# HGRN2 score levels on 64-column halves of TensorE, the diagonal as its own product on the same halves, the last level with half of the keys

## Chip, core and metric

The kernel runs on one core of a Trainium2 chip. The metric is the device time of one launch in microseconds (us). Three runs of the kernel before gave 2126.46 to 2127.39 us, median 2127.11.

## What is computed

Two layers of a decoder trunk, 512 tokens, width 1024, all in float32. Each layer has a SwiGLU network, a mixer, and a second SwiGLU network, with RMS norms around each. The mixer has one projection into everything it needs, a gated linear recurrence with four heads (HGRN2), a sliding-window attention with eight heads, and a gated sum of the two. The change lies in the recurrence. Per head, with keys and queries of 128 channels, the reference computes in chunks of 64 tokens:

```python
def step(state, inp):
    qb, kb, vb, gb = inp
    G = jnp.cumsum(gb, axis=2)
    o_inter = jnp.einsum('bhtd,bhde->bhte', qb * jnp.exp(G), state)
    diff = G[:, :, :, None, :] - G[:, :, None, :, :]
    decay = jnp.exp(jnp.where(causal[:, :, None], diff, -jnp.inf))
    scores = jnp.einsum('bhtd,bhtsd,bhsd->bhts', qb, decay, kb)
    o = o_inter + jnp.einsum('bhts,bhse->bhte', scores, vb)
    G_last = G[:, :, -1:, :]
    new_state = (jnp.exp(G_last[:, :, 0, :])[..., None] * state
                 + jnp.einsum('bhsd,bhse->bhde', kb * jnp.exp(G_last - G), vb))
    return new_state, o
```

So the score of query t and key s is a sum over channels of q(t) k(s) times the product of the forget gates f between s and t, for every s up to t.

## The kernel before

Activations lie with features on the 128 partitions and 512 tokens along the free dimension. Weights stream from DRAM in tiles of 128 x 1024 (`Stream`). ACT casts each tile to a rounded part `whi` (L321), and DVE (L328), or a DMA that POOL issues (L326), makes the rest `wlo`. A product of the large layers is then three matmuls (`mm3`). All matmuls go through `mm` (L115), all transposes through L122.

PE's instructions keep the order in which the program issues them. The other engines' orders are made by a scheduler. The program's own planner `Order` mixes the attention and the recurrence, which are generators, into the stream of weight products. It adds up an estimated PE time `order.t`. When a generator yields a delay from the table `WAIT`, it becomes due that much later, and the next call of `poll` after that runs it to its next yield. So PE does projections while DVE and ACT prepare the next product of a head.

PSUM has eight banks, of 512 float32 columns on 128 partitions each: five called `acc` (projections) and three called `aux` (everything small), each handed out in turn. Tiles of 128 x 512 in SBUF are called `s` (61 of them).

`recurrence_scores` (L938) makes one head's scores, which `mixer` calls through `head` and `run`. `q` and `kz` are a head's queries and keys, `f` the gates, `qa` starts as q times f. `TT` = 4 blocks of 128 tokens are worked on at the same time. Its steps:

- Diagonal (L945 to L952): four products of 128 keys by 128 queries, of which only the diagonal is wanted. DVE multiplies by the identity (L949) and writes the score tile `sd`.
- Levels b = 1, 2, 4, 8, 16, 32, taken in three pairs (L991). At level b, every second group of b queries meets the group of b keys just before it. `meet(b)` multiplies the odd groups of `qa` (L984) and the even groups of `kz` (L986) by products of gates, and halves the list of products `prod` (L988). `mv` holds three lots of 64 query columns for each block: those of level b, those of level 2b, and those of level 2b with a further gate for the far half of the keys (L1000). One product for each block (L1006) has 128 keys as the stationary operand and these 192 columns as the moving one. Two blocks fill a bank, so a pair of levels takes two `aux` banks. `place` (L970 to L976) then copies the wanted entries into `sd` with a mask, three times for each bank.
- Level 64 (L1016 to L1025): the second 64 queries of each block against all 128 keys, and a masked copy that keeps the first 64 keys.
- Then products between blocks (L1030 and L1041), which the change leaves as they are.

`run` multiplies the scores with the values into one bank, normalizes, gates and transposes. Heads 0 and 1 run beside the attention's projections, heads 2 and 3 later in the same mixer. In `attend`, the products at L1137 and L1189 already work on halves of the array.

Of the kernel before, what the change touches and what calls it, by code (L numbers as in the profile page):

```python
# [7 lines left out]
F32 = mybir.dt.float32  # L8
F32R = mybir.dt.float32r
I32 = mybir.dt.int32  # L10
AF = mybir.ActivationFunctionType
ALU = mybir.AluOpType
# [3 lines left out]
P = 128  # L16
# [4 lines left out]
TT = S // P  # L21
# [7 lines left out]
MASKS = [(m, n) for b in LEVELS[:-1:2] for m, n in ((b, b), (2 * b, 2 * b), (2 * b, b))] + [(64, 64)]  # L29
SLOTS = 61  # L30

WAIT = dict(
    early=0.0, first=0.0, spread=2300.0, squares=1700.0, lay=34500.0, laid=770.0, normed=7600.0, final=2600.0,
    head=2600.0, diag=0.0, level=1720.0, chunks=1270.0, blocks=350.0, norm=2370.0, gate=8000.0,
    values=1200.0, scores=2000.0, exp=9000.0, shares=4500.0, turn=1900.0, turned=3000.0, rest=1200.0, lent=3500.0, apart=4000.0, block=2000.0, pair=4000.0, att0=1260.0, att1=12300.0,
)
W32, WS, AHEAD, TAIL, PLAIN, FIRST, EARLY, LATE = 4, 6, 3, 4, 4, 7, 4, 8
# [8 lines left out]
def trunk(ctx: ExitStack, tc: tile.TileContext, xin, wall, gains, lbT, hgain, sinks, c_dist, c_mask, c_ident, out):  # L46
    nc = tc.nc
    cp = ctx.enter_context(tc.tile_pool(name="cp", bufs=1))
    sb = ctx.enter_context(tc.tile_pool(name="sb", bufs=1))
# [9 lines left out]
    def nm(s):  # L59
        seq[0] += 1  # L60
        return f"{s}_{seq[0]}"

    def big(dt=F32, shape=None):
        return sb.tile(shape or [P, S], dt, tag="s", name=nm("s"), bufs=SLOTS)
# [7 lines left out]
    def aux():  # L72
        return ps.tile([P, S], F32, tag="aux", name=nm("aux"), bufs=3)

    def const(shape, name, dt=F32):
        return cp.tile(shape, dt, tag=name, name=name)
# [35 lines left out]
    order = Order()  # L112

    def mm(o, lhsT, rhs, start, stop):
        nc.tensor.matmul(o, lhsT, rhs, start=start, stop=stop)  # L115
        n = 1
        for d in rhs.shape[1:]:
            n *= d
        order.t += max(n / 2.4, 27.0) * 4 if rhs.dtype == F32 else max(n / 2.4, 107.0)

    def transpose(o, src):
        nc.tensor.transpose(o, src, ident)  # L122
# [15 lines left out]
    p = aux()  # L138
    for _ in range(15):
        mm(p[:, :P], ones, ones, True, True)  # L140
# [12 lines left out]
    class Stream:  # L153
# [195 lines left out]
        def next(self, n=1, uses=1):  # L349

            c = self.c
            assert c + n <= 8
            it = self.need(self.cur)
            it.left += n * (uses - 1)
            self.c = (c + n) % 8
            if self.c == 0:
                self.cur += 1
            return it, n, it.hi[:, c * P : (c + n) * P], it.lo[:, c * P : (c + n) * P]
# [18 lines left out]
    def mm3(o, st, mv, start, stop):  # L377

        mm(o, st[0], mv[0], start, False)
        mm(o, st[0], mv[1], False, False)  # L380
        mm(o, st[1], mv[0], False, stop)
# [556 lines left out]
    def recurrence_scores(q, f, kz, box):  # L938

        qa = big()
        nc.vector.tensor_tensor(qa, q, f, op=ALU.mult)
        sd = big(F32, [P, TT, P])
        p0 = aux()  # L945
        for c in range(TT):
            cs = slice(c * P, (c + 1) * P)
            mm(p0[:, cs], kz[:, cs], q[:, cs], True, True)
        nc.vector.tensor_tensor(  # L949
            sd, p0.rearrange("p (c t) -> p c t", c=TT), ident.unsqueeze(1).to_broadcast([P, TT, P]), op=ALU.mult  # L950
        )
        yield WAIT["diag"]  # L952
        pr = big()
        prod, off = f, 0

        def halves(t, b):

            v = t.rearrange("p (n two b) -> p n two b", two=2, b=b)
            return v[:, :, 0, :], v[:, :, 1, :]

        def odd(t, b):
            return t.rearrange("p (c n two b) -> p c n two b", c=TT, two=2, b=b)[:, :, :, 1, :]

        def dense(t, b):
            return t.rearrange("p c (n b) -> p c n b", b=b)

        def spread(v, b):
            return v.to_broadcast([P, v.shape[1], b])

        def place(b, m, src, c):  # L970

            nc.vector.copy_predicated(
                sd.rearrange("p c (n two b) -> p c n two b", two=2, b=b)[:, c, :, 1, :],
                mask[:, m, :].rearrange("p (n b) -> p n b", b=b).unsqueeze(1).to_broadcast([P, 2, 64 // b, b]),
                dense(src, b),
            )  # L976

        def meet(b):

            nonlocal prod, off  # L980
            n = S // (2 * b)
            pv = prod.rearrange("p (n two) -> p n two", two=2)
            kv, qw = halves(kz, b)[0], halves(qa, b)[1]
            nc.vector.tensor_tensor(qw, qw, spread(pv[:, :, 0:1], b), op=ALU.mult)  # L984
            yield
            nc.vector.tensor_tensor(kv, kv, spread(pv[:, :, 1:2], b), op=ALU.mult)  # L986
            nxt = pr[:, off : off + n]
            nc.vector.tensor_tensor(nxt, pv[:, :, 0], pv[:, :, 1], op=ALU.mult)  # L988
            prod, off = nxt, off + n

        for i, b in enumerate(LEVELS[:-1:2]):  # L991


            mv = sb.tile([P, TT, 192], F32, tag="tt", name=nm("mv"), bufs=2)
            nc.scalar.copy(dense(mv[:, :, :64], b), odd(qa, b))
            first = meet(b)
            next(first)
            nc.scalar.copy(dense(mv[:, :, 64:128], 2 * b), odd(qa, 2 * b))
            way = prod.rearrange("p (c n four) -> p c n four", c=TT, four=4)[:, :, :, 1:2]
            nc.vector.tensor_tensor(  # L1000
                dense(mv[:, :, 128:], 2 * b), odd(qa, 2 * b), way.to_broadcast([P, TT, P // (4 * b), 2 * b]), op=ALU.mult
            )
            yield WAIT["pair"]
            lv = [aux()[:, :384].rearrange("p (c t) -> p c t", c=2) for _ in range(2)]
            for c in range(TT):
                mm(lv[c // 2][:, c % 2, :], kz[:, c * P : (c + 1) * P], mv[:, c, :], True, True)  # L1006
            next(first, None)
            for _ in meet(2 * b):
                pass
            for j, v in enumerate(lv):  # L1010
                c = slice(2 * j, 2 * j + 2)
                place(b, 3 * i, v[:, :, :64], c)
                place(2 * b, 3 * i + 1, v[:, :, 64:128], c)
                place(2 * b, 3 * i + 2, v[:, :, 128:], c)
            yield WAIT["level"]
        b = LEVELS[-1]  # L1016
        lv = aux()
        for c in range(TT):
            mm(lv[:, c * b : (c + 1) * b], kz[:, c * P : (c + 1) * P], qa[:, c * P + b : (c + 1) * P], True, True)
        for _ in meet(b):  # L1020
            pass
        v = lv[:, :256].rearrange("p (c t) -> p c t", c=TT)
        for j in range(2):
            c = slice(2 * j, 2 * j + 2)
            place(b, len(MASKS) - 1, v[:, c, :], c)  # L1025
        yield WAIT["level"]

        s1 = big(F32, [P, 2, P])
        p1 = aux()
        for i, (s, t) in enumerate(((0, 1), (2, 3))):  # L1030
            mm(p1[:, i * P : (i + 1) * P], kz[:, s * P : (s + 1) * P], qa[:, t * P : (t + 1) * P], True, True)
        for s, t in ((0, 1), (2, 3)):
            ks, qt = kz[:, s * P : (s + 1) * P], qa[:, t * P : (t + 1) * P]
            nc.vector.tensor_scalar(ks, ks, prod[:, t : t + 1], None, op0=ALU.mult)
            nc.vector.tensor_scalar(qt, qt, prod[:, s : s + 1], None, op0=ALU.mult)
        nc.scalar.copy(s1, p1[:, : 2 * P].rearrange("p (c t) -> p c t", c=2))
        yield WAIT["chunks"]

        s2 = big(F32, [P, 2, 2 * P])
        p2 = aux()  # L1040
        for s in range(2):  # L1041
            mm(p2[:, s * 256 : (s + 1) * 256], kz[:, s * P : (s + 1) * P], qa[:, 256:512], True, True)
        nc.scalar.copy(s2, p2.rearrange("p (c t) -> p c t", c=2))

        def block(s, t):
            if s == t:
                return sd[:, s, :]
            if (s, t) in ((0, 1), (2, 3)):
                return s1[:, s // 2, :]
            return s2[:, s, (t - 2) * P : (t - 1) * P]  # L1050

        box.append(block)
        yield WAIT["blocks"]

    def mixer(l, pre, nxt):
# [3 lines left out]
        def head(i, ph, pq):  # L1059
# [8 lines left out]
            def run():  # L1068
                yield WAIT["head"]
                box = []  # L1070
                yield from recurrence_scores(q, f, k, box)
                if len(vs) < TT:
                    while len(vs) < TT:
# [196 lines left out]
    for l in range(DEPTH):  # L1270
        for n in (0, 2, 4):
# [5 lines left out]
            else:  # L1277
                p = FIRST if l + n == 0 else PLAIN
# [10 lines left out]
    ident = const([P, P], "ident")  # L1289
    nc.sync.dma_start(ident, c_ident)  # L1290
    dist = const([P, 256], "dist")
    nc.sync.dma_start(dist, c_dist)
    mask = const([P, len(MASKS), 64], "mask", I32)
    nc.sync.dma_start(mask, c_mask)
    lb_in = const([P, DEPTH, H], "lb_in")
    nc.sync.dma_start(lb_in, lbT)
    hgh = const([P, DEPTH, P], "hgh")
# [136 lines left out]
```

## Time and profile before

| | us |
|---|---|
| median of three runs | 2127.11 |
| profiled execution, first to last instruction | 2123.9 |
| PE busy | 2110.6 |
| DVE busy | 1573.4 |
| ACT busy | 1119.0 |
| PE waits for other engines, in total | 9.1 |

The profiler records one execution. Busy time is the union of an engine's instructions. A matmul's record begins when it is issued and ends, by a model, when its last result is written, so records of successive matmuls overlap; what one costs is seen in the distance between starts. PEld is the loading of stationary operands. A float32 product leaves two such records, and a product of the rounded parts leaves one. In a row such as `128*64 128x512`, the first pair is the rows and columns of the array that are used (keys' channels by stationary columns), the second the moving operand. A bracket at the end of a row is idle time before it and what ended it. The recurrence's levels of heads 0 and 1 lie at 387 to 433 us in the first layer and 1437 to 1483 us in the second, those of heads 2 and 3 at 517 to 574 us and 1567 to 1624 us. The granted clock of TensorE was 0.999 over the span.

### The profile page before, as it was taken

The page shows a single profiled execution, that of the slowest core. Times are in us where ns is not written, and L with a number is a line of the kernel's source. Part 1 is how long each engine was busy: PE and PEld are TensorE (multiplying, and loading weights), DVE is VectorE, ACT ScalarE, POOL GpSimd, SP SyncE. Part 2 cuts the span into 40 slices and gives each one's busy share as a digit, 9 for nine tenths or more (in the row PEclk, how much of TensorE's full clock was granted, in tenths as well). Part 3 has the DMA queues.
Part 4 walks back from the last instruction along what each step waited for, and adds up shares of the span by engine and source line. Part 5 has one row for each costly group of instructions (what it writes and reads, how often), then busy time and mean ns, then how long its engine had stood idle before and what let it go on. Part 6 is the DMA issues. An engine that isn't in the chain of part 4 may idle for free.

```text
span 2123.9 us, 34765 instructions
## 1 busy us (share of the span) xinstructions
PE 2110.6 (99%) x13293; PEld 1898.1 (89%) x13293; DVE 1573.4 (74%) x2793; ACT 1119.0 (53%) x1884; POOL 152.2 (7%) x180
## 2 busy tenths in 40 slices
PE   9999999999999999999999999999999999999998
PEld 8899988887888999998899998898778989999987
DVE  5877886768776777789587778767687757777884
ACT  7555555346445555556455556453554545555562
POOL 0011000000000011110001110000000000111000
PEclk9999999999999999999999999999999999999999
DMA  8677663221236357774447775632122463677751
GB/s 251 149 185 182 167 181 118 92 67 64 66 100 208 120 125 176 182 197 123 153 113 177 183 183 141 197 119 80 60 70 60 124 194 110 149 180 182 185 158 51
DMA packets 146870, 298.48 MB, mean 141 GB/s; under 512 B 15664, under 2 KB 73488, under 8 KB 146704
## 3 DMA queue, kind: packets, MB, share of 16 engines
q1 hardware_dynamic: 121216, 228.31, 32.7%
q0 software_dynamic: 25344, 67.91, 18.6%
q8 instruction: 104, 1.70, 0.3%
q14 instruction: 62, 0.51, 0.1%
q10 hardware_dynamic: 144, 0.05, 0.0%
HBM read 213.58 MB, written 14.73 MB: 107 GB/s over the span
## 4 chain that ended last, share of the span: by engine, by line
PE 75%; DVE 7%; ACT 3%; issue 1%; DMA 1%; SPq 0%; ACTq 0%; DVEq 0%
PE acc L115 55%; PE aux L115 19%; DVE s L398 1%; PE aux L122 1%; ACT whi L321 1%; DVE wlo L283 1%; DMA w<-wall 1%; DVE wlo L328 1%; PE acc L122 1%; ACT s L397 1%; DVE tt L265 0%; DVE w L264 0%; DVE s L273 0%; DVE w L274 0%; ACT whi L278 0%
## 5 line engine op out<-in xcount | busy, mean ns | idle before, releaser
L115 PE MATMUL acc<-s,whi 128*128 128x256 f32 (+1 forms) x4968 | 1068.8, 312 | 0.7 <-DVE s L901 0.7
L115 PEld LDWEIGHTS acc<-s,whi 128*128 128x128 f32 x4968 | 810.1, 191 | 48.7 <-issue 3.7
L115 PE MATMUL acc<-s,wlo 128*128 128x256 f32 (+1 forms) x2484 | 770.2, 310 | 0.1
L115 PEld LDWEIGHTS acc<-s,wlo 128*128 128x128 f32 x2484 | 474.1, 191 | 26.0 <-DVE wlo L328 0.4
L321 ACT CAST whi<-w 128x1024 fp32r<-128x1024 f32 (+1 forms) x341 | 316.6, 947 | 242.0 <-PE aux L115 100.2
L115 PE MATMUL acc<-whi,s 128*128 128x512 f32 x1264 | 414.5, 394 | 0.0
L321 ACT CAST whi<-tt 128x1024 fp32r<-128x1024 f32 x154 | 161.4, 1048 | 337.7 <-DVE tt L315 199.5
L328 DVE TENSOR_TENSOR wlo<-w,whi 128x1024 fp32r<-128x1024 f32 (+1 forms) x181 | 218.5, 1216 | 135.3 <-ACT whi L321 131.6
L115 PEld LDWEIGHTS acc<-whi,s 128*128 128x128 f32 x1264 | 237.1, 188 | 55.7 <-issue 3.2
L328 DVE TENSOR_TENSOR wlo<-tt,whi 128x1024 fp32r<-128x1024 f32 x154 | 188.1, 1222 | 101.6 <-ACT whi L321 101.6
L326 POOL DMA_DIRECT2D wlo<-w x160 | 138.2, 865 | 1723.5 <-ACT wlo L325 1363.1
L115 PE MATMUL acc<-wlo,s 128*128 128x512 f32 x632 | 246.7, 390 | 1.2 <-DVE wlo L283 1.2
L115 PE MATMUL aux<-s,whi 128*128 128x256 f32 x1232 | 225.1, 283 | 0.0
L115 PE MATMUL aux<-whi,s 128*128 128x512 f32 x592 | 196.7, 390 | 0.0
L115 PEld LDWEIGHTS aux<-s,whi 128*128 128x128 f32 x1232 | 192.2, 192 | 0.0
L115 PE MATMUL aux<-s,wlo 128*128 128x256 f32 x616 | 174.3, 283 | 0.0
L115 PEld LDWEIGHTS acc<-wlo,s 128*128 128x128 f32 x632 | 118.8, 188 | 25.5 <-DVE wlo L283 2.4
L115 PEld LDWEIGHTS aux<-whi,s 128*128 128x128 f32 x592 | 111.2, 188 | 22.9
L325 ACT ACTIVATE wlo<-w 128x1024 fp32r<-128x1024 f32 (+1 forms) x160 | 129.8, 844 | 0.0
L397 ACT CAST s<-s 128x512 fp32r<-128x512 f32 (+1 forms) x164 | 88.4, 580 | 75.8 <-DVE s L456 72.2
L115 PEld LDWEIGHTS aux<-s,wlo 128*128 128x128 f32 x616 | 118.3, 192 | 0.0
L115 PE MATMUL aux<-wlo,s 128*128 128x512 f32 x296 | 115.2, 389 | 0.0
(182 smaller groups left out, 2189.1 us busy)
## 6 DMA issues: line engine op xcount, KB each, us to landing
w<-wall SPq DMA_DIRECT2D x267, 512.0 KB, 3.7
wlo<-w POOLq DMA_DIRECT2D x83, 512.0 KB, 5.5
w<-wall SPq DMA_DIRECT2D x288, 128.0 KB, 3.4
wlo<-w POOLq DMA_DIRECT2D x77, 256.0 KB, 3.3
x_d<-s SPq DMA_DIRECT2D x48, 256.0 KB, 2.1
s<-x_d SPq DMA_DIRECT2D x48, 256.0 KB, 5.5
w<-wall SPq DMA_DIRECT2D x34, 256.0 KB, 3.2
s<-wall SPq DMA_DIRECT2D x64, 128.0 KB, 3.7
```

The lines of the kernel that those rows point to most:

```text
L115: nc.tensor.matmul(o, lhsT, rhs, start=start, stop=stop)
L122: nc.tensor.transpose(o, src, ident)
L283: nc.vector.tensor_tensor(it.lo[:, h[c]], w[c], it.hi[:, h[c]].bitcast(F32), op=ALU.subtract)
L321: i = nc.scalar.copy(it.hi[:, c], w[:, c])
L325: nc.scalar.mul(it.lo[:, c], w[:, c], -1.0)
L326: nc.gpsimd.dma_start(it.lo[:, c].bitcast(F32), w[:, c], accum_op=ALU.add)
L328: nc.vector.tensor_tensor(it.lo[:, c], w[:, c], it.hi[:, c].bitcast(F32), op=ALU.subtract)
L397: nc.scalar.copy(hi, src)
L398: nc.vector.tensor_tensor(lo, src, hi.bitcast(F32), op=ALU.subtract)
```

## The change

- The 128 keys of a block are cut into two halves of 64. Half h is the stationary operand of a product that writes PSUM partitions 64h to 64h + 63, with the 32 query columns of each lot that lie in that half: 96 columns instead of 192, `mv` having eight blocks of 64 tokens. All of a pair's results lie in one bank.
- The diagonal's product has 64 keys by 64 queries for each half, is issued with the first pair's products in one burst, and is multiplied by the identity in two instructions, one for each half, after that burst. Its own yield (`diag`) is gone.
- `place` takes one half of the partitions and all four blocks at a time.
- Level 64 takes the first 64 keys alone as its stationary operand; ACT copies the result without a mask.
- POOL sets one quarter of `sd` to zero, which the diagonal's product no longer writes.
- The mask is loaded in two halves, and the last level has none.
- The planner counts half the time for a float32 product with 64 stationary columns and fewer than 256 moving ones.

In the order in which the changed kernel is built, the first burst of heads 0 and 1 stands 12 weight matmuls before the place of the first pair's burst. The other bursts of heads 0 and 1 follow with the same number of weight matmuls between them as before (27 and 6 in turn). POOL's eight memsets stand between its DMAs of the first SwiGLU network and those of the branch gates. SP has one more DMA, the second half of the mask.

```diff
@@ -116,7 +116,10 @@
-        order.t += max(n / 2.4, 27.0) * 4 if rhs.dtype == F32 else max(n / 2.4, 107.0)
+        if rhs.dtype == F32:
+            order.t += max(n / 2.4, 27.0) * (2 if lhsT.shape[1] == 64 and n < 256 else 4)
+        else:
+            order.t += max(n / 2.4, 107.0)
@@ -942,14 +945,7 @@
         qa = big()
         nc.vector.tensor_tensor(qa, q, f, op=ALU.mult)
         sd = big(F32, [P, TT, P])
-        p0 = aux()
-        for c in range(TT):
-            cs = slice(c * P, (c + 1) * P)
-            mm(p0[:, cs], kz[:, cs], q[:, cs], True, True)
-        nc.vector.tensor_tensor(
-            sd, p0.rearrange("p (c t) -> p c t", c=TT), ident.unsqueeze(1).to_broadcast([P, TT, P]), op=ALU.mult
-        )
-        yield WAIT["diag"]
+        nc.gpsimd.memset(sd[64:, :, :64], 0.0)
         pr = big()
         prod, off = f, 0
 
@@ -959,21 +955,23 @@
             return v[:, :, 0, :], v[:, :, 1, :]
 
         def odd(t, b):
-            return t.rearrange("p (c n two b) -> p c n two b", c=TT, two=2, b=b)[:, :, :, 1, :]
+            return t.rearrange("p (x n two b) -> p x n two b", x=2 * TT, two=2, b=b)[:, :, :, 1, :]
 
         def dense(t, b):
-            return t.rearrange("p c (n b) -> p c n b", b=b)
+            return t.rearrange("p x (n b) -> p x n b", b=b)
 
         def spread(v, b):
             return v.to_broadcast([P, v.shape[1], b])
 
-        def place(b, m, src, c):
-
-            nc.vector.copy_predicated(
-                sd.rearrange("p c (n two b) -> p c n two b", two=2, b=b)[:, c, :, 1, :],
-                mask[:, m, :].rearrange("p (n b) -> p n b", b=b).unsqueeze(1).to_broadcast([P, 2, 64 // b, b]),
-                dense(src, b),
-            )
+        def place(b, m, lv, g):
+
+            for h in range(2):
+                r = slice(64 * h, 64 * h + 64)
+                nc.vector.copy_predicated(
+                    sd[r].rearrange("p c (x n two b) -> p c x n two b", x=2, two=2, b=b)[:, :, h, :, 1, :],
+                    mask[r, m, :].rearrange("p (n b) -> p n b", b=b).unsqueeze(1).to_broadcast([64, TT, 32 // b, b]),
+                    dense(lv[r, :, g * 32 : g * 32 + 32], b),
+                )
 
         def meet(b):
 
@@ -991,38 +989,47 @@
         for i, b in enumerate(LEVELS[:-1:2]):
 
 
-            mv = sb.tile([P, TT, 192], F32, tag="tt", name=nm("mv"), bufs=2)
-            nc.scalar.copy(dense(mv[:, :, :64], b), odd(qa, b))
+            mv = sb.tile([P, 2 * TT, 96], F32, tag="tt", name=nm("mv"), bufs=2)
+            nc.scalar.copy(dense(mv[:, :, :32], b), odd(qa, b))
             first = meet(b)
             next(first)
-            nc.scalar.copy(dense(mv[:, :, 64:128], 2 * b), odd(qa, 2 * b))
-            way = prod.rearrange("p (c n four) -> p c n four", c=TT, four=4)[:, :, :, 1:2]
+            nc.scalar.copy(dense(mv[:, :, 32:64], 2 * b), odd(qa, 2 * b))
+            way = prod.rearrange("p (x n four) -> p x n four", x=2 * TT, four=4)[:, :, :, 1:2]
             nc.vector.tensor_tensor(
-                dense(mv[:, :, 128:], 2 * b), odd(qa, 2 * b), way.to_broadcast([P, TT, P // (4 * b), 2 * b]), op=ALU.mult
+                dense(mv[:, :, 64:96], 2 * b), odd(qa, 2 * b), way.to_broadcast([P, 2 * TT, 16 // b, 2 * b]), op=ALU.mult
             )
             yield WAIT["pair"]
-            lv = [aux()[:, :384].rearrange("p (c t) -> p c t", c=2) for _ in range(2)]
+            p0 = None if i else aux()
+            lv = aux()[:, : TT * 96].rearrange("p (c t) -> p c t", t=96)
             for c in range(TT):
-                mm(lv[c // 2][:, c % 2, :], kz[:, c * P : (c + 1) * P], mv[:, c, :], True, True)
+                for h in range(2):
+                    r, x = slice(64 * h, 64 * h + 64), 2 * c + h
+                    if not i:
+                        mm(p0[r, x // 2 * 64 : x // 2 * 64 + 64], kz[:, x * 64 : x * 64 + 64], q[:, x * 64 : x * 64 + 64], True, True)
+                for h in range(2):
+                    r, x = slice(64 * h, 64 * h + 64), 2 * c + h
+                    mm(lv[r, c, :], kz[:, x * 64 : x * 64 + 64], mv[:, x, :], True, True)
             next(first, None)
             for _ in meet(2 * b):
                 pass
-            for j, v in enumerate(lv):
-                c = slice(2 * j, 2 * j + 2)
-                place(b, 3 * i, v[:, :, :64], c)
-                place(2 * b, 3 * i + 1, v[:, :, 64:128], c)
-                place(2 * b, 3 * i + 2, v[:, :, 128:], c)
+            if i == 0:
+                for h in range(2):
+                    r = slice(64 * h, 64 * h + 64)
+                    nc.vector.tensor_tensor(
+                        sd[r, :, r], p0[r, : TT * 64].rearrange("p (c t) -> p c t", c=TT),
+                        ident[r, r].unsqueeze(1).to_broadcast([64, TT, 64]), op=ALU.mult,
+                    )
+            place(b, 3 * i, lv, 0)
+            place(2 * b, 3 * i + 1, lv, 1)
+            place(2 * b, 3 * i + 2, lv, 2)
             yield WAIT["level"]
         b = LEVELS[-1]
         lv = aux()
         for c in range(TT):
-            mm(lv[:, c * b : (c + 1) * b], kz[:, c * P : (c + 1) * P], qa[:, c * P + b : (c + 1) * P], True, True)
+            mm(lv[:b, c * b : (c + 1) * b], kz[:, c * P : c * P + b], qa[:, c * P + b : (c + 1) * P], True, True)
         for _ in meet(b):
             pass
-        v = lv[:, :256].rearrange("p (c t) -> p c t", c=TT)
-        for j in range(2):
-            c = slice(2 * j, 2 * j + 2)
-            place(b, len(MASKS) - 1, v[:, c, :], c)
+        nc.scalar.copy(sd[:b, :, b:], lv[:b, : TT * b].rearrange("p (c t) -> p c t", c=TT))
         yield WAIT["level"]
 
         s1 = big(F32, [P, 2, P])
@@ -1290,8 +1297,9 @@
     nc.sync.dma_start(ident, c_ident)
     dist = const([P, 256], "dist")
     nc.sync.dma_start(dist, c_dist)
-    mask = const([P, len(MASKS), 64], "mask", I32)
-    nc.sync.dma_start(mask, c_mask)
+    mask = const([P, len(MASKS) - 1, 32], "mask", I32)
+    for h in range(2):
+        nc.sync.dma_start(mask[64 * h : 64 * h + 64], c_mask[64 * h : 64 * h + 64, :-1, 32 * h : 32 * h + 32])
     lb_in = const([P, DEPTH, H], "lb_in")
     nc.sync.dma_start(lb_in, lbT)
     hgh = const([P, DEPTH, P], "hgh")
```

More of the change, by code (lines that the diff above doesn't have):

```diff
@@ L32 @@
 WAIT = dict(
-    early=0.0, first=0.0, spread=2300.0, squares=1700.0, lay=34500.0, laid=770.0, normed=7600.0, final=2600.0,
-    head=2600.0, diag=0.0, level=1720.0, chunks=1270.0, blocks=350.0, norm=2370.0, gate=8000.0,
+    first=0.0, spread=2300.0, squares=1700.0, lay=34500.0, laid=770.0, normed=7600.0, final=2600.0,
+    head=2600.0, level=1720.0, chunks=1270.0, blocks=350.0, norm=2370.0, gate=8000.0,
     values=1200.0, scores=2000.0, exp=9000.0, shares=4500.0, turn=1900.0, turned=3000.0, rest=1200.0, lent=3500.0, apart=4000.0, block=2000.0, pair=4000.0, att0=1260.0, att1=12300.0,
```

## The prediction

> **What bounds the kernel now.** I read the page's first two parts, then who PE waited for, then PE's groups with shapes kept apart, then PE's timeline around each short product of the recurrence.
>
> ```profile
> span 2123.9 us, 34765 instructions
> PE 2110.6 (99%) x13293; PEld 1898.1 (89%) x13293; DVE 1573.4 (74%) x2793; ACT 1119.0 (53%) x1884; POOL 152.2 (7%) x180
> ```
>
> PE is busy for all but 13.3 us of the span. So time taken from PE's own list comes off the end one for one, as long as nobody makes PE wait instead. The list of waits shows how near that is:
>
> ```profile
> PE aux L115 <- DVE s L972: 3.2, 2, 1.6
> PE acc L122 <- DVE s L727: 2.9, 1, 2.9
> ```
>
> The first row is in the code that changes: twice (once in each layer) a product of the recurrence waited 1.6 us for a PSUM bank that `place` (L972, DVE) still read. No row names a DMA.
>
> PE's groups for the products that change, and for two that already use part of the array:
>
> ```profile
> L115 PE MATMUL aux<-mv,s 128*128 128x192 f32 x192 | 35.6, 326 | 3.2 <-DVE s L972 3.2
> L115 PE MATMUL aux<-s,s 128*128 128x128 f32 x256 | 32.4, 274 | 0.0
> L115 PE MATMUL aux<-s,s 128*64 128x512 f32 x56 | 13.8, 607 | 0.0
> L115 PE MATMUL aux<-s,s 128*128 128x64 f32 x64 | 8.0, 268 | 0.0
> L115 PE MATMUL aux<-s,s 64*128 64x128 f32 x48 | 3.6, 280 | 0.0
> ```
>
> Each float32 product leaves two records: 8 heads (4 per layer) x 3 pairs x 4 blocks = 96 products, x192. The means of 270 to 600 ns are latencies and overlap; a price needs the starts in the timeline. I take a burst from its start to where the regular stream of three 512-column matmuls is back in step, less that stream's own time.
>
> ```profile
> 387.34 1.05 PE L115 MATMUL aux<-s,s 128*128 128x128 f32 x8
> ...
> 388.92 0.62 PE L115 MATMUL acc<-s,whi 128*128 128x512 f32 x2
> ...
> 399.33 0.81 PE L115 MATMUL aux<-mv,s 128*128 128x192 f32 x4
> 401.74 0.89 PE L115 MATMUL aux<-mv,s 128*128 128x192 f32 x4 [1.60 <-DVE s L972]
> ...
> 418.09 0.62 PE L115 MATMUL acc<-s,whi 128*128 128x512 f32 x2
> ...
> 418.77 1.46 PE L115 MATMUL aux<-mv,s 128*128 128x192 f32 x8
> ...
> 420.78 0.62 PE L115 MATMUL acc<-s,whi 128*128 128x512 f32 x2
> ...
> 424.16 1.00 PE L115 MATMUL aux<-s,s 128*128 128x64 f32 x8
> ...
> 425.74 0.62 PE L115 MATMUL acc<-s,whi 128*128 128x512 f32 x2
> ```
>
> 418.09 to 418.77 is one undisturbed group of three: 0.68 us. Between each burst's start and the last row of its part lies one such group. So the diagonal (128 columns) costs 388.92 - 387.34 - 0.68 = 0.90, a pair of levels (192 columns) 420.78 - 418.77 - 0.68 = 1.33, the last level (64 columns) 425.74 - 424.16 - 0.68 = 0.90. Eight records of 192 columns last 1.46 and four 0.81: 0.1625 us a record, 0.846 ns a column. The 64 columns cost as much as the 128, so something other than columns bounds them:
>
> ```profile
> L115 PEld LDWEIGHTS aux<-mv,s 128*128 128x128 f32 x192 | 32.4, 189 | 5.7 <-issue 3.7
> L115 PEld LDWEIGHTS aux<-s,s 128*64 128x64 f32 x56 | 3.3, 135 | 6.3 <-issue 4.9 <-ACT s L397 0.7 <-DVE s L988 0.7
> ```
>
> 64 weight columns fewer make a load 189 - 135 = 54 ns shorter. Estimate: 0.054 us per 64 columns, 0.108 for 128, and 8 x 0.108 = 0.87 is close to the 0.90 of both.
>
> **Do halves of the array run side by side?** The attention's value product (`po` in `attend`) already sends pairs of 64-column products to the two column halves, into one bank. The scores use two row halves.
>
> ```profile
> 482.83 0.40 PE L115 MATMUL acc<-whi,s 128*128 128x512 f32 x1
> 483.16 1.94 PE L115 MATMUL aux<-s,s 128*64 128x512 f32 x8
> ...
> 485.60 0.62 PE L115 MATMUL acc<-whi,s 128*128 128x512 f32 x2
> 434.40 0.40 PE L115 MATMUL acc<-whi,s 128*128 128x512 f32 x1
> 434.73 0.89 PE L115 MATMUL aux<-s,s 64*128 64x128 f32 x12
> ...
> 436.12 0.63 PE L115 MATMUL acc<-whi,s 128*128 128x512 f32 x2
> ```
>
> Three regular matmuls (0.68) lie in each stretch. The column pairs cost 485.60 - 482.83 - 0.68 = 2.09. One after the other, eight records of 512 columns would take 8 x 0.433 = 3.46; two at a time they take 1.73. So they do overlap, and the rest, 0.36, is what a burst on halves pays to go in and come out (full-array bursts pay about 0.03). [...]
>
> **The change on PE, per head.** Times are columns or weight loads, whichever is longer, for a pair of halves, plus 0.36 for each burst.
> - Diagonal and first pair are now one burst. Diagonal: 4 blocks x 2 records x 0.054 = 0.43. Levels: 8 x 96 columns x 0.846 ns = 0.65. With 0.36: 1.44, against 0.90 + 1.33 = 2.23. Saves 0.79.
> - Second and third pair: 0.65 + 0.36 = 1.01 against 1.33. Saves 0.32 each.
> - Last level: half of the keys, so 64 weight columns, but one half of the array alone, no partner: 8 x 0.054 + 0.36 = 0.79 against 0.90. Saves 0.11.
>
> That is 0.79 + 0.64 + 0.11 = 1.54 a head, 12.3 us for eight. The extreme for an entry and exit is the other row above: 1.04 for twelve records on row halves, six slots of at least 0.108, leaves 0.39. I keep 0.36; 0.03 more in 32 bursts would be 1.0 us.
>
> **Banks and the wait at L972.** Before, a pair took two of three banks, so the second head's burst always needed one back. Now a pair takes one, except the first, which takes two (`p0` and `lv`): two heads need four, and head 1's `lv` waits until head 0's diagonal has been read twice. From the end of head 0's burst DVE has ahead of that release one diagonal half, two updates of k, one of q, one `prod`, the other half. What those take is seen here:
>
> ```profile
> 402.28 0.46 DVE L984 TENSOR_TENSOR s<-s,s 128x256 f32<-128x256 f32 x1
> 402.67 0.43 DVE L986 TENSOR_TENSOR s<-s,s 128x256 f32<-128x256 f32 x1
> 403.01 0.28 DVE L988 TENSOR_TENSOR s<-s 128x128 f32<-128x128 f32 x1
> 403.21 0.42 DVE L986 TENSOR_TENSOR s<-s,s 128x256 f32<-128x256 f32 x1
> 403.55 1.90 DVE L972 COPY_PREDICATED s<-mask,aux 128x128 f32<-128x128 int32 x6
> ```
>
> Start to start: 0.39 + 0.34 + 0.20 + 0.34 = 1.27, and two 256-element halves at 0.34: 1.95, against two groups of PE work (1.36) before head 1's burst. The wait becomes about 0.6 instead of 1.6: 2.0 us saved over two layers, between 3.2 (none left) and -2 (each 1 us longer than before). Behind the waiting product on PE stand the projections, so the whole wait counts. DVE is then ready for the next level 1.95 + 1.9 (six places) + 3.9 (the same for head 1) + 0.6 (a 512-element split that stands between) + 4 x 0.34 (q of both heads, `mv`) = 9.7 us after head 0's burst. PE fills 1.4 (two groups) + 0.6 + 1.44 + 9 groups, 6.1 = 9.5: 0.2 late, 0.4 for both layers. So the waits give 1.6, and with 12.3 the sum is 14 us.
>
> **What is taken at nothing.**
>
> ```profile
> L972 DVE COPY_PREDICATED s<-mask,aux 128x128 f32<-128x128 int32 x160 | 47.7, 344 | 7.0 <-PE aux L115 6.9
> L949 DVE TENSOR_TENSOR s<-aux,ident 128x512 f32<-128x512 f32 x8 | 5.5, 690 | 4.8 <-PE aux L115 4.8
> L1036 ACT COPY s<-aux 128x256 f32<-128x256 f32 x8 | 3.0, 374 | 22.7 <-PE aux L115 22.7
> 385.00:432.00 47.00, 45.40 (x234) 39.20 (x233) 39.42 (x112) 16.05 (x30) 0.00 (x0) 1.00 0.22 73
> mask<-c_mask SPq DMA_DIRECT2D x1, 320.0 KB, 5.4
> L972 DVE COPY_PREDICATED s<-mask,aux x160: 266/297/512, 399.5 to 1616.9; 128x128 f32<-128x128 int32 x160
> ```
>
> `place` runs on half the partitions but with 128 elements on each, as before: 18 a head instead of 20. That takes 0.7 off DVE; the diagonal in two halves (2 x 0.42 for 0.69) adds 0.15. ACT gains one 256-element copy (0.37) and was busy 16 of 47 us. The memset is on POOL, which did nothing in that window; its size is not in the trace, between nothing and the 0.7 of a 512-element DVE operation, and the first `place` that needs it comes several us later. The mask comes in two loads behind one another on SP, ahead of three small constants and the weights: one more issue near 11 us, the mask first read at 399.5 us, and PE never waited for a weight load. Uncovered it would be 1 us, once.
>
> **Rivals.**
> 1. *DVE becomes the bound in the levels of heads 0 and 1.* For: it is busy 39.4 of 47.0 us there, and would need some 38.3 of 43.1. Against: from the second pair on, without a diagonal, the same count gives DVE some 7 us for PE's 8.5 (1.4 + 1.01 + 6.1). If it takes everything that heads 0 and 1 save in both layers (4 x 1.54 = 6.2) and the 1.6: 2121.
> 2. *Records cannot be issued fast enough.* Twelve records on row halves cost 1.04, less 0.36 is 0.057 a record, and nothing in the trace is proven faster. At 0.057 a burst of 32 records costs 2.18 (saves 0.05), of 16 records 1.27 (saves 0.06 each), the last 0.82 (0.08): 0.25 a head, 2.0 us, with 1.6 of waits 2123.5: no change by measure. Against: those records had 128 weight columns to load, 0.108 a slot of two, which explains 0.054 by itself. [...]
> 3. *The halves do not overlap at 64 and 96 columns* because a half's second record holds the queue before the other half's first. Then the first burst takes 16 x 0.054 + 16 x 0.081 + 0.36 = 2.52 (+0.29), the next two 1.66 (+0.33 each), the last -0.11: +0.84 a head, +6.7 us, less 1.6: 2132, slower. It decides as soon as less than a third of the overlap is had (0.84 of 2.38 a head). Against: at 512 columns the same pattern of records overlaps fully.
>
> **The numbers.** The profiled execution spans 2123.9; the runs' median is 2127.1, so 3.2 us lie around the span. 2123.9 - 14 = 2110, and with 3.2: 2113. Chances: forecast with its own range 2108 to 2118, 0.68; rival 1 0.14; rival 2 0.08; rival 3 0.06; something unseen 0.04. The range 2107 to 2122 takes in no wait left at all on one side and rival 1 on the other. A measurement tells 0.2% (4.3 us): faster is below 2122.9, slower above 2131.4. Forecast, rival 1 and part of the rest: faster 0.84; rival 2 and the rest: same 0.09; slower 0.07.
>
> **What would show it.** Right: in PE's timeline a first-pair burst costs 1.4 to 1.5 and a later one 1.0; records of the two halves start within 10 to 20 ns of each other; `place` as releaser is gone or below 1.5 us in PE's waits, and the diagonal's line shows about 0.6 twice; busy PE falls by 11 to 13 us. Wrong: bursts above 1.3 for a later pair (rival 2 or 3, told apart by whether the halves start together), or PE's waits for DVE and ACT above 6 us between a layer's projections (rival 1).

## The result, and the profile after

The changed kernel takes 2124.04 us (median of 19 runs, 2121.33 to 2125.81) against 2127.11 (19 runs, 2126.29 to 2128.21): 0.9984 of the time before, interval 0.9978 to 0.9990. The forecast was 2113, and its range, 2107 to 2122, does not hold the median. The gain is 3 us where 14 were expected, so some 11 us are to be found. The profiled execution took 2123.18 us, of which 2121.4 is the span.

The first two parts of its page:

```profile
span 2121.4 us, 35292 instructions
PE 2100.9 (99%) x13549; PEld 1874.6 (88%) x13549; DVE 1585.9 (75%) x2785; ACT 1120.3 (53%) x1892; POOL 154.6 (7%) x188
```

PE is busy 9.7 us less than before (2110.6), but the rest of the span, 13.3 us before, is now 20.5. Did the bursts become as cheap as forecast? PE's timeline of the changed kernel, each pair of lines from the last regular matmul ahead of a burst to the first whole group behind it (start, duration, line, operation):

```profile
391.72 0.39 PE L115 MATMUL acc<-s,wlo 128*128 128x512 f32 x1
...
394.12 0.63 PE L115 MATMUL acc<-s,whi 128*128 128x512 f32 x2
...
418.57 0.39 PE L115 MATMUL acc<-s,wlo 128*128 128x512 f32 x1
418.89 0.88 PE L115 MATMUL aux<-mv,s 128*64 128x96 f32 x16
...
420.50 0.62 PE L115 MATMUL acc<-s,whi 128*128 128x512 f32 x2
...
420.96 0.39 PE L115 MATMUL acc<-s,wlo 128*128 128x512 f32 x1
...
422.69 0.62 PE L115 MATMUL acc<-s,whi 128*128 128x512 f32 x2
```

Four regular matmuls (4 x 0.227 = 0.91) lie in each stretch. First burst with the diagonal: 2.40 - 0.91 = 1.49. A later pair: 1.93 - 0.91 = 1.02. Last level: 1.73 - 0.91 = 0.82. Together 1.49 + 2 x 1.02 + 0.82 = 4.35 a head against 5.76 before (0.90 + 3 x 1.32 + 0.90): 1.41 saved, 11.3 us for eight heads. In the trace's single records of the burst at 418.89 the two halves of a pair start 6 to 7 ns apart, and the next pair 0.076 us behind the second half. So the products did what was hoped. The list of PE's waits shows who took the gain back (engine, tile, releaser: us in total, times, longest):

```profile
PE aux L115 <- ACT mv L996: 4.6, 2, 2.3
...
PE aux L115 <- DVE s L1042: 2.7, 2, 1.4
PE aux L115 <- DVE s L984: 1.3, 2, 0.7
...
PE aux L115 <- DVE s L1018: 0.6, 2, 0.3
```

9.2 us of waits in the recurrence instead of 3.2. The last row, the bank, had been expected (about 0.6 each time; it is 0.3), and 0.2 of the first row. The largest is at the second pair of head 0, in each layer. ACT's copy is named, but it waits for DVE's `qa`, so DVE's timeline shows why, with the group of all places below it:

```profile
393.34 0.41 DVE L1018 TENSOR_TENSOR s<-aux,ident 64x256 f32<-64x256 f32 x1
...
394.97 0.43 DVE L1018 TENSOR_TENSOR s<-aux,ident 64x256 f32<-64x256 f32 x1
395.43 2.80 DVE L970 COPY_PREDICATED s<-mask,aux 64x128 f32<-64x128 int32 x6
398.25 0.43 DVE L984 TENSOR_TENSOR s<-s,s 128x256 f32<-128x256 f32 x1
...
400.80 2.79 DVE L970 COPY_PREDICATED s<-mask,aux 64x128 f32<-64x128 int32 x6
403.59 0.69 DVE L404 SCALAR_TENSOR_TENSOR s<-acc,s 128x512 fp32r<-128x512 f32 x1
```

```profile
L970 DVE COPY_PREDICATED s<-mask,aux 64x128 f32<-64x128 int32 x144 | 49.6, 345 | 3.7
```

Six places of 128 elements take 2.80 us; before, six of 128 elements took 1.90 on twice the partitions. A single one lasts no longer (the mean is 345 ns, before 344), but they no longer overlap: from the end of one to the start of the next the single records show 13 to 31 ns, where before the next started some 217 ns ahead of that end. The mean of the group cannot show this; the time from start to start does.

PE's timeline at the end of that wait, and the granted clock behind it (columns of the second view: stretch, length, busy time and instructions of PE, weight loads, DVE, ACT, POOL, then granted clock, DMA share, GB/s):

```profile
402.77 0.39 PE L115 MATMUL acc<-s,wlo 128*128 128x512 f32 x1
405.44 0.88 PE L115 MATMUL aux<-mv,s 128*64 128x96 f32 x16 [2.27 <-ACT mv L996]
...
408.63 1.55 PE L115 MATMUL aux<-mv,s 128*64 128x96 f32 x16
```

```profile
406.82:410.23 3.41, 3.41 (x22) 2.34 (x20) 2.93 (x10) 0.31 (x3) 0.00 (x0) 0.50 0.00 0
```

Some 1.4 us after the wait of 2.27 us the clock is halved for 3.41 us, and a burst that takes 0.88 takes 1.55. That costs another 1.7 us (half of 3.41) in this execution. The account: 11.3 saved by the bursts, 6.0 lost to more waits, and 1.7 to the clock leave 3.6; the span fell by 2.5. The other 1.1 us are not traced in full. A wait costs a little more than the list says: the stretch with the bank's wait of 0.31 (394.58 to 397.52) is 2.94 long, against 2.40 without a wait, so 0.54. The list also has a new wait of 0.83 us for ACT's `whi` (L324) ahead of the first regular matmul, but that matmul starts at 6.92 us, against 6.83 before, because the products with `ones` ahead of it end earlier: it explains some 0.1 us.

### The profile page after: what moved, and what is told of

Same layout as the page of the kernel before. It is cut to its first block, busy times and chain, and to the rows that moved or that the text cites. A ratio compares the mean times of both kernels' runs of the same rounds, so it can differ in the third digit from the quotient of the medians.

```text
span 2121.4 us, 35292 instructions
## 1 busy us (share of the span) xinstructions
PE 2100.9 (99%) x13549; PEld 1874.6 (88%) x13549; DVE 1585.9 (75%) x2785; ACT 1120.3 (53%) x1892; POOL 154.6 (7%) x188
## 4 chain that ended last, share of the span: by engine, by line
PE 72%; DVE 9%; ACT 3%; issue 2%; DMA 1%; SPq 1%; ACTq 0%; DVEq 0%; POOLq 0%
PE acc L115 52%; PE aux L115 18%; DVE s L401 1%; DVE s L970 1%; PE aux L125 1%; ACT whi L324 1%; DMA w<-wall 1%; DVE wlo L286 1%; ACT s L400 1%; SPq L241 1%; PE acc L125 1%; DVE wlo L331 1%; DMA wlo<-w 1%; ACT whi L281 1%; DVE tt L268 0%
## 5 line engine op out<-in xcount | busy, mean ns | idle before, releaser
L324 ACT CAST whi<-w 128x1024 fp32r<-128x1024 f32 (+1 forms) x341 | 316.7, 947 | 251.9 <-PE aux L115 101.3
L324 ACT CAST whi<-tt 128x1024 fp32r<-128x1024 f32 x154 | 161.4, 1048 | 341.3 <-DVE tt L318 202.2
```

Of the source, the lines that this page charges most:

```text
L324: i = nc.scalar.copy(it.hi[:, c], w[:, c])
```

## The experiments

Each ratio below is against runs of the kernel before on the same chip.

**No places at all.** The three calls of `place` for the pairs are left out, so the levels' scores are missing from the result.

```diff
-            place(b, 3 * i, lv, 0)
-            place(2 * b, 3 * i + 1, lv, 1)
-            place(2 * b, 3 * i + 2, lv, 2)
```

> The changed kernel without the masked copies (place) of the three pairs; the levels' scores are left out of the result, all matmuls stay. Theory A (the shorter products on PE are as cheap as forecast, and DVE, held up by the masked copies, makes PE wait): PE's waits for DVE and ACT in the recurrence fall from 9.2 us to under 1.5 us, TensorE's granted clock does not drop, and the time falls to 2112 to 2114 us. Rival B (the waits come from the bank that the first burst needs back and from the diagonal that moved behind it): the 2.3 us wait at the second level goes or shrinks but over 3 us of waits stay, 2117 or more. Rival C (something outside the recurrence took the gain, the split mask load or POOL's memset): the time stays above 2120.

Measured: 2111.46 us (2110.54 to 2111.84), 0.9927 (0.9913 to 0.9940), half a microsecond below what was expected. No wait of PE in the recurrence is left on the list. So PE's saving is real, and DVE's part around `place` is what takes it back. Whether it is the number of places or their form is not told by this.

**Compact scores.** The scores of both halves go to a tile `sc` of 128 partitions by 4 x 64, so that a lot is placed by one instruction on all partitions, 9 a head; the diagonal is one multiplication by a folded identity `idh`; ACT copies the halves into `sd`.

```diff
+        sc = big(F32, [P, TT, 64])
-            for h in range(2):
-                r = slice(64 * h, 64 * h + 64)
-                nc.vector.copy_predicated(sd[r]...
+            nc.vector.copy_predicated(
+                sc.rearrange("p c (n two b) -> p c n two b", two=2, b=b)[:, :, :, 1, :],
+                mask[:, m, :].rearrange("p (n b) -> p n b", b=b).unsqueeze(1).to_broadcast([P, TT, 32 // b, b]),
+                dense(lv[:, :, g * 32 : g * 32 + 32], b),
+            )
...
+        for h in range(2):
+            r = slice(64 * h, 64 * h + 64)
+            nc.scalar.copy(sd[r, :, r], sc[r])
...
+        nc.vector.tensor_tensor(idh, ident[:, :64], ident[:, 64:], op=ALU.add)
```

> The changed kernel with the two halves' scores collected in one compact tile of 128 x 4 x 64, so that place and the diagonal's product are one instruction on all 128 partitions instead of two on halves (three masked copies for a pair, not six), and ACT copies the two halves out at the end; nothing is left out. Theory A: masked copies take 22 us of DVE instead of 50, PE's waits in the recurrence fall to under 3 us, time 2112 to 2116. Rival B: the bank wait of 0.3 us shrinks, the others stay, 2120 or more. Rival D (the planner's delays are simply too short now that the bursts are shorter, and DVE's chain of multiplications alone is longer than them): waits of 4 us or more stay, 2117 or more.

Measured: 2117.17 us (2116.07 to 2117.92), 0.9954 (0.9942 to 0.9966): 1 us above theory A's range and inside that of rival D, but the waits that rival D needs are missing. The list of PE's waits begins with one that has nothing to do with the recurrence, and holds none from there:

```profile
PE acc L115 <- DVE s L501: 3.7, 1, 3.7
```

It lies at 13.4 us. DVE made `idh` there, and waited 7.1 us for the load of `ident`. So the kernel gained in one place and paid in another.

**Later due times.** The places stay as they are; the planner lets more weight matmuls pass between the bursts of a head.

```diff
-            yield WAIT["level"]
+            yield WAIT["level"] + (3500.0, 0.0, 1400.0)[i]
...
-    head=2600.0, level=1720.0, chunks=1270.0, blocks=350.0, norm=2370.0, gate=8000.0,
+    head=2600.0, level=1720.0, chunks=2900.0, blocks=350.0, norm=2370.0, gate=8000.0,
```

> The changed kernel with longer delays in the planner (3.5 us after the first pair, 1.4 us after the third, 1.63 us after the products between blocks), so PE does more projections before it comes to the products that waited; DVE's work is the same. Theory A as a matter of latency alone: the waits of 2.3, 0.65 and 1.35 us in each layer go, time 2113 to 2117. If DVE lacks throughput rather than time, the waits move to later products and the time stays at 2121 to 2125.

Measured: 2116.67 us (2116.40 to 2117.44), 0.9953 (0.9940 to 0.9965). Of PE's waits in the recurrence these three rows are left, and one of 0.4:

```profile
PE aux L115 <- DVE s L1018: 0.6, 2, 0.3
PE aux L115 <- DVE s L986: 0.6, 2, 0.3
PE aux L115 <- ACT mv L996: 0.5, 2, 0.3
```

So DVE is not full; it is late, between two bursts that the planner set too close for it. The attention paid for the delay with a new row of 1.9 us in two waits (L1175).

**What stops the overlap, first try.** A tail behind the changed kernel's last work: eight masked copies and eight multiplications in a row on all 128 partitions, on the lower 64, on the upper 64, and in turn.

> The changed kernel with a tail of DVE instructions that measure the masked copy by itself, eight in a row each: on all 128 partitions, on the lower 64, on the upper 64, on lower and upper in turn, and the same four with a multiplication of 256 elements. The tail adds some 25 us to the span; only its spacing is of interest. Theory A1 (a DVE instruction does not overlap with its neighbour when they lie on different halves of the partitions): in a row on one half, and on all, successive masked copies start about 0.29 us apart, in turn 0.47; multiplications 0.34 and 0.43. Rival A2 (any masked copy on 64 partitions is slower): 0.45 on each half alone too. Rival A3 (the new access pattern is slower, whatever the partitions): 0.45 on all 128 too.

DVE's timeline of that tail, the four rows of copies:

```profile
2118.68 3.75 DVE L1372 COPY_PREDICATED s<-mask,aux 128x128 f32<-128x128 int32 x8
...
2126.21 3.68 DVE L1372 COPY_PREDICATED s<-mask,aux 64x128 f32<-64x128 int32 x8
...
2133.71 3.77 DVE L1372 COPY_PREDICATED s<-mask,aux 64x128 f32<-64x128 int32 x8
...
2141.50 3.69 DVE L1372 COPY_PREDICATED s<-mask,aux 64x128 f32<-64x128 int32 x8
```

All alike, 0.44 to 0.48 us from start to start. The experiment missed its aim: in the first three rows every copy wrote what the one before it had written, and started only when that one was over or nearly so (a copy lasts 0.44 us, median), whatever its partitions. These rows show what such a dependence costs, and the fourth, where the halves alternate, is no slower, so the two causes cannot be told apart here. One detail pointed on: a small instruction behind the last copy started 187 to 196 ns before that copy's end where the copy began on partition 0, and 13 to 14 ns after it where it began on partition 64.

**The same with independent writes.** Copies to eight places, multiplications around four.

> The changed kernel with a tail after its last work: eight masked copies of 128 elements that write eight different places, then eight multiplications of 256 elements that go around four places, first all on 128 partitions, then on the lower 64, then on the upper 64, then lower and upper in turn. Unlike in the earlier tail, hardly one depends on the one before it. Theory H (only a change of the starting half stops the overlap): copies start 0.2 to 0.3 us apart on 128, on lower and on upper alike, and 0.44 to 0.48 in turn; multiplications 0.34 and in turn 0.43 or more. Rival U (the upper half never overlaps): upper alone 0.44 or more too. Rival W (64 partitions never overlap): lower alone 0.44 or more too.

```profile
2121.39 1.67 DVE L1374 COPY_PREDICATED s<-mask,aux 128x128 f32<-128x128 int32 x8
2122.97 2.76 DVE L1381 TENSOR_TENSOR s<-s 128x256 f32<-128x256 f32 x8
2125.66 1.67 DVE L1374 COPY_PREDICATED s<-mask,aux 64x128 f32<-64x128 int32 x8
2127.24 2.76 DVE L1381 TENSOR_TENSOR s<-s 64x256 f32<-64x256 f32 x8
2130.01 1.76 DVE L1374 COPY_PREDICATED s<-mask,aux 64x128 f32<-64x128 int32 x8
2131.65 2.82 DVE L1381 TENSOR_TENSOR s<-s 64x256 f32<-64x256 f32 x8
2134.50 2.53 DVE L1374 COPY_PREDICATED s<-mask,aux 64x128 f32<-64x128 int32 x8
2137.06 3.58 DVE L1381 TENSOR_TENSOR s<-s 64x256 f32<-64x256 f32 x8
```

On all partitions, on the lower and on the upper half alike: 0.20 us between copies, 0.335 between multiplications. In turn: 0.31 to 0.33 and 0.45. Both rivals fall: of the three, only the change of the starting half stops the overlap. The expected 0.44 to 0.48 for copies in turn was too high: a lone copy lasts 0.29 here and 0.44 in the first pair, so starting only after its end costs more there. (That it lasts longer there because it strides over the result was not tried.)

Starting on the two halves in turn, 64 partitions apart, against starting on one: 0.317 against 0.198 us from start to start for the copies, 0.450 against 0.335 for the multiplications. Other distances were not tried.

**Every place twice, on all partitions.** The compact kernel with each place issued again into a tile that nobody reads: 18 a head, as in the changed kernel (the lines are shown against the compact kernel). Its constant is made in the first recurrence head in the program's text.

```diff
-            nc.vector.copy_predicated(
-                sc.rearrange(...
+            for d in (sc, se):
+                nc.vector.copy_predicated(
+                    d.rearrange(...
```

> As the compact kernel with the constant made late, but every place is issued twice, the second time into a tile that nobody reads: 18 places a head as in the changed kernel, all on 128 partitions. Theory H (alternating halves of the partitions): the doubled places start 0.2 to 0.3 us apart, the six that follow the first pair take 1.3 to 1.9 us, TensorE's waits in the recurrence stay below 3 us in total, 2114 to 2117. Rival N (it is the number of places, 18 against 9 a head, whatever partitions they are on): six take 2.8 us again, waits of about 9 us, 2121 or more.

Measured: 2117.10 us (2116.65 to 2117.41), 0.9956 (0.9944 to 0.9968). DVE's group of places, and the six behind a first pair:

```profile
L977 DVE COPY_PREDICATED s<-mask,aux 128x128 f32<-128x128 int32 x144 | 37.5, 355 | 0.0
```

```profile
401.73 1.90 DVE L977 COPY_PREDICATED s<-mask,aux 128x128 f32<-128x128 int32 x6
```

As many places as in the changed kernel (144), as long each (355 ns, there 345), yet six take 1.90 instead of 2.80, and no wait of PE in the recurrence is left. The number of places is not the cause. The time is just above what was expected; the wait of 3.7 us at 13.3 us is still there (the scheduler had moved the constant back to the start).

**The compact kernel with a late constant.** The line for `idh` moved to the first recurrence head.

> The compact kernel again, with its one small constant (idh) made at the first recurrence head instead of at the start, where it made VectorE wait for the load of ident and TensorE 3.7 us behind it. Nothing is left out. Theory H (the halved places cost because each starts on another half of the partitions than the one before it, so that none overlaps its neighbour; compact places all start on partition 0): no wait of TensorE in the recurrence above 0.5 us, and the 3.7 us at the start gone against about 0.8 there: 2117.2 - 3 = 2113 to 2115. Rival L (the 3.7 us hid other waits, which come back): 2116 or more, with new waits on the list.

Measured: 2117.53 us (2116.18 to 2118.94), 0.9959 (0.9946 to 0.9971). A miss in the time: the scheduler put the instruction back to the start, and PE waited 4.4 us there. In the recurrence no wait of PE is left, as theory H has it.

```profile
16.81 0.22 DVE L954 TENSOR_TENSOR idh<-ident 128x64 f32<-128x64 f32 x1 [7.15 <-DMA ident<-c_ident]
```

**Places by half.** The changed kernel with the three places of the lower half first, then the three of the upper.

```diff
-        def place(b, m, lv, g):
-
-            for h in range(2):
+        def place(b, m, lv, g, h):
+
+            if True:
...
-            place(b, 3 * i, lv, 0)
-            place(2 * b, 3 * i + 1, lv, 1)
-            place(2 * b, 3 * i + 2, lv, 2)
+            for h in range(2):
+                place(b, 3 * i, lv, 0, h)
+                place(2 * b, 3 * i + 1, lv, 1, h)
+                place(2 * b, 3 * i + 2, lv, 2, h)
```

> The changed kernel with the six places of a pair in another order: the three of the lower half, then the three of the upper half. Nothing is left out. Theory H: two changes of the half per pair instead of six, but places of one half that write the same tile one behind another still wait for each other unless other work lies between them; so a small gain, 2119 to 2123, and lower places that follow full-width work overlap it by about 0.08 us or more while upper ones do not. Rival O (the order of halves does not matter, only that a place works on 64 partitions): 2123 to 2125 and every place stands free of its neighbours.

Measured: 2120.68 us (2120.27 to 2121.91, 8 runs), 0.9975 (0.9964 to 0.9985), as expected. DVE's timeline:

```profile
395.45 0.43 DVE L970 COPY_PREDICATED s<-mask,aux 64x128 f32<-64x128 int32 x1
395.70 0.44 DVE L986 TENSOR_TENSOR s<-s 128x256 f32<-128x256 f32 x1
396.07 0.42 DVE L970 COPY_PREDICATED s<-mask,aux 64x128 f32<-64x128 int32 x1
...
398.05 0.45 DVE L970 COPY_PREDICATED s<-mask,aux 64x128 f32<-64x128 int32 x1
398.53 0.43 DVE L984 TENSOR_TENSOR s<-s,s 128x256 f32<-128x256 f32 x1
398.97 0.45 DVE L970 COPY_PREDICATED s<-mask,aux 64x128 f32<-64x128 int32 x1
```

The lower place at 395.45, beside full-width work that also starts on partition 0, is followed 0.25 us after its start; the upper ones stand free (0.48 behind the one at 398.05, 0.44 from the multiplication to the one at 398.97). PE's longest wait behind head 0's first pair falls from 2.3 to 0.5; the 1.4 at head 2 stays. All waits in the recurrence fall from 9.2 to 7.4 us only; the profiled execution also has a clock of 1.00 from 403 to 408 us; a stretch at half clock like the changed kernel's is worth up to 1.7.

**The compact kernel without the wait at the start.** `idh` is pinned in DVE's written order, some 30 us into the kernel (the lines are shown against the compact kernel).

```diff
-        nc.vector.tensor_tensor(idh, ident[:, :64], ident[:, 64:], op=ALU.add)
+        pin(nc.vector.tensor_tensor(idh, ident[:, :64], ident[:, 64:], op=ALU.add))
```

> The compact kernel with its small constant held in the written order of VectorE, about 30 us into the kernel, where ident has long landed (in the two compact kernels before, the scheduler had moved it ahead, to where VectorE waited 7.1 us for that load and TensorE 3.7 to 4.4 us behind it). Nothing is left out. Theory H: the wait at 13.3 us is gone, no wait of TensorE in the recurrence, 2117.1 - 3.7 = 2113 to 2114.5. Rival L (that wait only took the place of others): 2116 or more, with about 3 us of waits elsewhere on the list.

Measured: 2110.45 us (2110.06 to 2111.46), 0.9922 (0.9909 to 0.9936): it beats both kernels, by 16.8 and by 13.6 us, and is below what was expected. Its page, and the two longest of PE's waits:

```profile
span 2108.3 us, 35246 instructions
PE 2097.8 (100%) x13549; PEld 1874.5 (89%) x13549; DVE 1550.5 (74%) x2706; ACT 1126.8 (53%) x1908; POOL 154.2 (7%) x188
```

```profile
PE acc L125 <- DVE s L730: 2.9, 1, 2.9
PE aux L115 <- DVE eps_t L138: 1.1, 1, 1.1
```

Both stand in the kernel before too. Against the compact kernel with the wait, 6.8 us in the profiled spans (2115.1 to 2108.3) went with a wait of 3.7: that wait was followed by a clock of half from 16.10 to 22.80 us, 6.70 us, worth up to 3.4 more.

## Why the prediction was wrong

- *Burst prices: right.* 1.49, 1.02 and 0.82 against 1.44, 1.01 and 0.79. The saving is 11.3 us for 12.3; the difference lies in these hundredths and in the 1.33 taken for a pair before, where the median over all 24 is 1.32. The entry and exit of 0.36 for each burst on halves carried over to 64 and 96 columns.
- *Records issued too slowly (rival 2): fell.* A later pair's 16 records cost 1.02 - 0.36 = 0.66, 0.041 us each, below the 0.057 of that rival. *Halves one after the other (rival 3): fell*, by the 6 to 7 ns between their starts.
- *The step that failed is "What is taken at nothing": `place` "with 128 elements on each, as before".* It let fewer places count as less DVE time and put 1.9 us for six of them into the next step, DVE ready 9.7 us after head 0's first burst and "0.2 late". The six took 2.8, because each starts on another half than the one before. From the end of head 0's first burst (393.34) to PE's next burst (405.44) 12.1 us passed. Of the 2.4 more, 2 x 0.9 are the places of the two heads. The rest, 0.6, is about 0.5 for the diagonal's halves and their neighbours, which are held in the same way (0.46 for 0.34, 0.29 for 0.20), and 0.3 for an update of `prod` of head 1 (at 398.59) that the 3.9 did not count, less 0.2 elsewhere. PE itself needed 9.8, forecast 9.5. So the wait became 2.3 in each layer instead of 0.2, and 0.7 and 1.4 came at head 2, where the prediction had no wait at all.
- *The bank wait: right in place, half the size* (0.3 for 0.6).
- *Rival 1 came true in effect, not by its cause.* DVE became what PE waits for in the recurrence, 9.2 us over both layers against the 6 us named as its sign, and the time went past its 2121. It was argued from DVE's busy time. The doubled places show that the work would have fitted: it was the lost overlap, and the delays show that it was lateness, not load.
- *The clock was not in the sum.* One stretch of 3.41 us at half clock is 1.7 us.
- Without the held places the kernel is 3 us below the forecast (2110.45): the bank wait, of which 1.2 was to remain, is gone, as is the 0.4. Of PE's busy time, 12.8 us less than before, the bursts explain 11.3. Another 0.6 lies in the first 40 us (37.55 us busy instead of 38.15), where PE now waits 0.6 for `whi`. Some 0.5 more lies in the two bursts that waited for the bank before: each took a stretch of 4.07 us, 0.24 more than its listed wait of 1.60 and the 2.23 of a burst without one.

## What to carry to other kernels

Cutting an instruction into halves of the partitions was not free here even where each half had as many elements per partition as the whole had: six places took 2.80 us instead of 1.90. So look at the start-to-start time of its neighbours (0.317 us in turn, 0.198 on one half), and keep runs of VectorE work on one starting partition, or put the halves' data side by side so that one instruction covers both. When a burst on one engine is made shorter, time the other engine's chain between two bursts from end to end, instead of adding up its load. A new constant is part of a change too: where a scheduler may move its instruction ahead, it can wait for a load at the start (7.1 us here, and PE 3.7 behind it).

## What the runs showed that was not expected

- The loss of overlap: where the starting half changes in the changed kernel (393 to 404 us), a VectorE instruction starts 13 to 32 ns after the end of the one before it; on one starting half, with nothing to wait for, it starts some 70 to 220 ns ahead of that end there and in the kernel before.
- The clock: 2.27 us without work on PE were followed by 3.41 us at half clock; the equal wait of the second layer, 2.30 us, was not, and neither was the 1.60 us before. Waits of 3.7 and 4.4 us at the start in the first compact kernel and the one with a late constant were followed by half clock from 16.10 to 22.80 us and from 18.20 to 25.00. The clock's records in the changed kernel's trace start whole multiples of 3.413 us apart (at 4.05, 406.82, 410.23 and 2116.90 us: 118, 1 and 500 of them), and on that grid the three stretches around the waits are (columns as above; PE's busy time follows the length):

```profile
403.41:406.82 3.41, 1.39 (x19) 1.21 (x20) 3.40 (x12) 2.17 (x5) 0.00 (x0) 1.00 0.00 0
1451.30:1454.71 3.41, 2.07 (x10) 1.38 (x8) 3.26 (x8) 0.00 (x0) 0.00 (x0) 1.00 0.00 0
1454.71:1458.12 3.41, 2.44 (x24) 1.82 (x24) 3.09 (x12) 2.49 (x5) 0.00 (x0) 1.00 0.03 7
```

  The first wait lies mostly in one stretch, with 1.39 us of work, and the next stretch is halved. The second is split over two stretches, with 2.07 and 2.44, and nothing is halved. In the kernel before, on the grid of its own records (6.13 and 2118.98 us, 619 multiples apart), the stretches of the two waits of 1.60 us (from 398.66 and 1449.97) have 1.81 us of work each, and the next ones are at 1.00. So between the two waits of 2.27 and 2.30 us it is their place on the grid that differs, not their length; that the place decides is the author's estimate from these stretches. This may also be why the changed kernel's runs spread over 4.5 us while those of the kernel before spread over 1.9: its two fastest runs, 2121.33 and 2121.48, have a mean granted clock of 0.999, all others 0.997 or 0.998. That was not tried by itself.
